# Moving operands of a hybrid decoder step laid out in rows of 2304 bytes, with a 4 KB DMA ring for GpSimd

## The chip, the cores and the metric

The kernel runs on one core of a Trainium2 chip. The metric is the device time of one execution in microseconds (us); the median of three runs of the kernel before is 1835.51 us (1834.74 to 1837.76). The profile is one execution taken by the hardware profiler.

## What is computed

One step of a decoder layer for 256 prompt tokens and 8 sample tokens (264 columns), all in float32: an RMS norm, one large input projection, three groups of heads, an output projection, the residual and a final norm.

```python
h = rms_norm(x, norm_w)
z = h @ w_in                                   # 4096 x 14368
qa, ka, va, ga, ub, gb, qc, kc, vc, gc, ac, bc = split_cols(z)
oa = combine_patterns([dilated_pattern(...) for w, d in A_PATTERNS])   # attention, 8 heads
ob = pool_mix(...)                                                     # causal pooling
oc = rms_norm(gated_delta(...), delta_norm_w)                          # delta rule, 16 heads
mix = concatenate([oa * silu(ga), ob * silu(gb), oc * silu(gc)])
y = rms_norm(x + mix @ w_out, final_norm_w)
```

The caches of keys and values are also copied through, shifted by one row.

## The kernel before

Both projections run as one stream of TensorE work. An output tile has 128 rows and 264 columns (`NT`), and there are 113 tiles of the input projection and 32 of the output projection. Each sums over 32 contraction tiles, here called k tiles. To keep float32 accuracy, every operand is split in an upper part and a lower part in the type float32r: a k tile of an output tile takes three matmuls (upper weights by upper x, upper weights by lower x, lower weights by upper x), lines 540, 541 and 542 of `emit_main`. I call the three a triple. The first output tile, `ab`, takes two matmuls instead (L535 to L538).

The moving operand of a triple comes from `rhs`. In the input projection it is row k of the tiles `xh` (upper) and `xl` (lower), each of 32 rows of 264 floats, so a row has 1056 bytes and the next starts 1056 bytes on. In the output projection it is row k of the mixed heads: `mixc0` to `mixc15`, one tile of 2 x 264 floats (2112 bytes) for each head of the delta rule, and the 16 rows of `mix2`, also of 2112 bytes; in both the lower part lies 1056 bytes behind the upper part.

Where a row lies follows from the sizes of what is allocated before it in a partition of the on-chip memory. Before `xh` stand 16384 bytes of the ring in which GpSimd's DMA descriptors are kept, 128 bytes of constants, 8 weight tiles of 4096, 3 raw tiles of 8192, the arena of 11776 floats, `small` of 1600 floats and 16 tiles of 2112 bytes: 161152 bytes, which is 128 modulo 256. `xl` lies 33792 bytes behind it, also at 128. Since 1056 is 32 modulo 256, row k of `xh` and of `xl` starts at 128 + 32 k modulo 256: eight places, one after the other. By the same count `mixc0` starts at 127360 (128 modulo 256), each next tile 64 further, and `mix2` takes the place of `xl`. So the upper parts of the output projection start at 128, 192, 0 and 64 in turn, and their lower parts 32 behind. The weights' tiles start at 128 modulo 256 for every matmul, before and after.

ScalarE makes the upper part of the weights and VectorE the lower one, chunk by chunk (8 k tiles), from three raw buffers that SyncE (SP) loads; `HB = 4` chunks of split weights may be ready. All else (convolutions, the delta rule's chains, attention, pooling) is written as generators. `step` lets each go on as far as a table of estimated engine times (`Model`) says that VectorE and ScalarE have time beside the stream, and as far as `get_all` finds room in the arena. So the order of the instructions on all engines is fixed when the program is built; a different size of the arena can change it. SP issues nearly all DMAs in one queue, in that order. GpSimd issues twelve small loads of constants and states.

Of the kernel before, what the change touches and what calls it, by code (L numbers as in the profile page):

```python
# [11 lines left out]
P = 128  # L12
NP = 256            # prompt tokens
NB = 8              # sample tokens (one per sequence)
NT = NP + NB
NK = 32             # contraction tiles of the model width
KC = 8              # contraction tiles per chunk
# [10 lines left out]
def tile_plan():  # L28
    """Order of the output tiles of the input projection: (kind, index)."""
    plan = [("ab", 0)] + [("k", h) for h in range(CH)]  # L30
    for h in range(CH):
        plan += [("q", h), ("v", h), ("g", h)]
    for h in range(AH):
        plan += [("qa", h), ("ka", h), ("va", h), ("ga", h)]
    for g in range(4):
        plan += [("u", 2 * g), ("u", 2 * g + 1), ("gb", 2 * g), ("gb", 2 * g + 1)]
    return plan
# [37 lines left out]
class Model:  # L75
    """Estimated times (us) of the engines' queues, and of every column's last write and last use."""
# [7 lines left out]
    def span(self, ap):  # L84
        """The quarters of the partitions and the columns of a tile (the kernel's inputs and outputs are not followed)."""
# [31 lines left out]
    def op(self, eng, dur, outs, ins):  # L117
        t = max(self.t[eng], self.ready(outs, ins))
        # engines take turns at a PSUM bank
# [24 lines left out]
class Meter:  # L144
    """An engine, with an estimate of the time that its instructions take (us)."""
# [33 lines left out]
class Chain:  # L179
    """A generator, the estimated time at which its last step is through, and its products yet to be issued."""  # L180
# [10 lines left out]
class Builder:  # L191
# [17 lines left out]
    def setup_space(self):  # L209
# [4 lines left out]
        self.XH = self.xp.tile([P, NK, NT], F32R, tag="xh", name="xh")  # L214
        self.XL = self.xp.tile([P, NK, NT], F32R, tag="xl", name="xl")
        self.r1 = [self.r1p.tile([P, 2, NT], F32, tag=f"r1_{h}", name=f"xr{h}") for h in range(CH)]
# [29 lines left out]
    def get_all(self, *sizes):  # L246
        """All of them or none, so that no two chains wait for each other's space."""
# [42 lines left out]
    def due(self, loaded):  # L290
        """Until a load can be expected to be there."""
        while not self.free and loaded > max(self.model.t["v"], self.model.t["pe"]) + SOON:
            yield
# [5 lines left out]
    def lose(self, t):  # L299
        """Time for ScalarE's tables."""  # L300
        self.s.used += t
        self.model.t["s"] += t

# [1 line left out]
    def mm(self, out, lhsT, rhs, start=True, stop=True):  # L305
        """A side product: it is issued inside a later chunk of the stream."""
# [14 lines left out]
    def flush(self, every=True):  # L321
        """The side products whose operands can be expected to be there."""
# [34 lines left out]
    def setup_const(self):  # L357
        d = self.d
        small = self.pool.tile([P, 1600], F32, name="small")
# [37 lines left out]
    def late_const(self):  # L397
# [4 lines left out]
        # halves: silu(z) = (tanh(z/2) + 1) * z/2  # L402
        self.ts(self.cw, self.cw, 0.5, ALU.mult)
        # buffers of the delta-rule phase
# [12 lines left out]
    def setup_stream(self):  # L417
        self.chunks = []      # (m, first k tile, number of k tiles, load index, offset in the load's tiles)
        self.loads = []       # (m, first k tile, number of k tiles, last chunk served, place, load that frees it)
# [36 lines left out]
    def emit_loads(self, limit=None):  # L456
        """The loads whose place is free."""
# [48 lines left out]
    def rhs(self, m, k):  # L506
        if m < N_IN:
            return self.XH[:, k, :], self.XL[:, k, :]
        t = self.mix[k]
        return t[:, 0:NT], t[:, NT:2 * NT]  # L510

    def main_bank(self, m):
        """The PSUM bank of an output tile, and the tile that had it before."""
# [4 lines left out]
    def emit_main(self, n):  # L518
# [3 lines left out]
        for i in range(nk):  # L522
# [8 lines left out]
            if m == 0:  # L531
                # rows 0 to 63: W's upper part by x; rows 64 to 127: its lower part by x's upper part
# [16 lines left out]
    def split_x(self, k):  # L549
        x = self.r1[k // 2][:, k % 2, :]  # L550
        w = self.nw[:, k:k + 1]
        self.act(self.XH[:, k, :], x, AF.Copy, scale=w)
        self.stt(self.XL[:, k, :], x, w, self.XH[:, k, :].bitcast(F32), ALU.mult, ALU.subtract)

    def square_x(self, q):
        """Squares of four of the k tiles, summed into self.ssum."""
# [51 lines left out]
    def ev_conv(self, kind, h, ps):  # L608
# [31 lines left out]
        if kind == "k":  # L640
            r = self.r1p.tile([P, 2 * NT], F32, tag=f"r1_{h}", name=f"kt{h}")
# [18 lines left out]
    def ev_ab(self, ps):  # L660
# [13 lines left out]
        # a_log -> -exp(a_log)  # L674
# [47 lines left out]
    def decay(self, h, gcb, D):  # L722
        """D[j, t, i] = exp(gc_i - gc_j) for i >= j, else 0."""
# [58 lines left out]
    def invert(self):  # L782
        """T = (I + A)^-1 of the 128 diagonal 32 x 32 blocks, one block per partition."""
# [32 lines left out]
    def assemble(self, hb):  # L816
        """E = T^T of the 128 x 128 tiles, from its 32 x 32 diagonal blocks, in place of U."""
# [90 lines left out]
    def delta(self, h, R, kd, D, o, S, X, sq):  # L908
# [65 lines left out]
        # 128 eps (sum q^2 + eps)  # L974
# [19 lines left out]
        # the last reader of k, U and E has been issued: their place takes the head's output  # L994
        mt = self.r1p.tile([P, 2 * NT], F32R, tag=f"r1_{h}", name=f"mixc{h}")
# [7 lines left out]
    def put_mix(self, mt, base, m, c0, c1):  # L1003
        hi, lo = mt[:, base + c0:base + c1], mt[:, base + NT + c0:base + NT + c1]
# [6 lines left out]
    def sample_tab(self):  # L1011
        """Columns by (head, sequence), then rows on all partitions: e^g, k2 e^g beta, k beta."""
# [72 lines left out]
    def sample_end(self):  # L1085
# [22 lines left out]
        for h in range(CH):  # L1108
# [3 lines left out]
            self.tt(mt[:, NT + NP:2 * NT], m, mt[:, NP:NT].bitcast(F32), ALU.subtract)  # L1112
# [56 lines left out]
    def have(self, k, buf):  # L1169
        """Row tile k of the mixed heads; those of attention come in two parts."""  # L1170
# [4 lines left out]
    def split_mix(self, k):  # L1175
# [3 lines left out]
        self.tt(t[:, NT:2 * NT], m.ap, t[:, 0:NT].bitcast(F32), ALU.subtract)  # L1179
# [164 lines left out]
    def ev_y(self, m, ps):  # L1344
        if m == 0:
            self.y = self.xp.tile([P, NK, NT], F32, tag="xh", name="y")
# [26 lines left out]
    def finish_early(self):  # L1373
        """What the last norm needs of the tiles but one."""
# [20 lines left out]
    def step(self, free=False):  # L1395
        """Each side chain goes on by a step, as far as VectorE and ScalarE have time beside the stream."""
# [87 lines left out]
    def build(self):  # L1484
# [8 lines left out]
        # TensorE's clock rises while it is busy  # L1493
# [19 lines left out]
        for n in range(len(self.chunks)):  # L1513
# [22 lines left out]
            if m >= N_IN:  # L1536
                if m == N_IN and c == 0:
                    self.mix2 = self.xp.tile([P, CH, 2 * NT], F32R, tag="xl", name="mix2")
# [59 lines left out]
ARENA = 11776  # L1598
# [8 lines left out]
# the first output tiles go side by side through the contraction, while x comes in  # L1607
# [4 lines left out]
# pieces of the caches' copy per load of weights: keys' tiles, delta rule, attention, pooling, output  # L1612
# [137 lines left out]
```

## Time and profile before

| | |
|---|---|
| time, median of 3 runs | 1835.51 us (1834.74 to 1837.76) |
| span of the profiled execution | 1828.2 us; its own time is not given apart from the span, and the median lies 7.3 us above the span |
| TensorE busy | 1801.3 us, 99% of the span |
| VectorE, ScalarE, GpSimd busy | 71%, 47%, 11% |
| chain of work that ended last | TensorE 88%, VectorE 5%, DMA 4% |
| granted TensorE clock from 130 to 1800 us | 1.00 (the 2.4 GHz level) |

Busy time of TensorE counts every matmul from its start to its modelled end, and successive matmuls overlap, so 99% tells that one always follows another and not how fast they follow. How fast is read from the starts.

### The profile page before, as it was taken

How to read it: one execution, taken by the hardware profiler on the slowest of the kernel's cores; microseconds unless marked ns; L12 is line 12 of the kernel's file. 1: busy time of each engine (PE TensorE's matmuls, PEld its weight loads, DVE VectorE, ACT ScalarE, POOL GpSimd, SP SyncE). 2: the span in 40 equal slices, each digit the busy share in tenths (PEclk: the TensorE clock that was granted, in tenths of full speed). 3: DMA queues.
4: the chain of work that ended last, by engine and by line, in shares of the span. 5: the costliest groups of instructions: out<-in, count | busy, mean ns of one | idle time of the engine just before them, and what ended most of it. 6: DMA issues, size and time to landing. Idle time of an engine off the chain costs nothing.

```text
span 1828.2 us, 38217 instructions
## 1 busy us (share of the span) xinstructions
PE 1801.3 (99%) x15120; PEld 1790.3 (98%) x15120; DVE 1298.7 (71%) x3155; ACT 850.3 (47%) x1442; POOL 192.8 (11%) x504
## 2 busy tenths in 40 slices
PE   9999999999999999999999999999999999999996
PEld 9999999999999999999999999999999999999995
DVE  7987879668789788787877778676655654444444
ACT  7644444455455455455544443434333444444442
POOL 1132560421011101111000000000000000000000
PEclk9999999999999999999999999999999999999998
DMA  9788897656787888879888888889888798888873
GB/s 322 263 289 295 272 234 260 237 198 234 262 327 269 286 305 313 304 267 319 323 312 306 313 308 297 284 283 333 306 299 288 274 339 302 295 294 303 297 240 118
DMA packets 109380, 519.66 MB, mean 284 GB/s; under 512 B 25408, under 2 KB 35872, under 8 KB 70272
## 3 DMA queue, kind: packets, MB, share of 16 engines
q1 hardware_dynamic: 108624, 516.71, 80.5%
q8 instruction: 118, 1.93, 0.4%
q0 software_dynamic: 432, 0.50, 0.1%
q14 instruction: 62, 0.51, 0.1%
q10 hardware_dynamic: 144, 0.02, 0.0%
HBM read 499.67 MB, written 152.50 MB: 357 GB/s over the span
## 4 chain that ended last, share of the span: by engine, by line
PE 88%; DVE 5%; DMA 4%; issue 1%; ACT 1%; SPq 1%; DVEq 0%; ACTq 0%
PE mps L540 27%; PE mps L541 27%; PE mps L542 27%; PE sps L307 4%; DVE arena L174 3%; DMA raw<-win 3%; DVE wl L174 2%; PE sps L311 1%; PE sps L541 1%; PE sps L540 1%; PE sps L542 1%; SPq L158 1%; DVE y L174 1%; DMA o_ds<-arena 0%; ACT wh L174 0%
## 5 line engine op out<-in xcount | busy, mean ns | idle before, releaser
L540 PE MATMUL mps<-xh,wh 128*128 128x264 f32 x3456 | 995.3, 288 | 2.0 <-ACT wh L174 2.0
L542 PE MATMUL mps<-xh,wl 128*128 128x264 f32 x3456 | 979.9, 284 | 1.7 <-DVE wl L174 1.6
L174 DVE TENSOR_TENSOR wl<-raw,wh 128x1024 fp32r<-128x1024 f32 (+1 forms) x581 | 704.5, 1214 | 389.7 <-ACT wh L174 382.4
L541 PE MATMUL mps<-xl,wh 128*128 128x264 f32 x3456 | 980.2, 284 | 0.0
L174 ACT CAST wh<-raw 128x1024 fp32r<-128x1024 f32 (+2 forms) x586 | 604.8, 1036 | 611.2 <-PE mps L541 471.7
L540 PEld LDWEIGHTS mps<-xh,wh 128*128 128x128 f32 x3456 | 652.1, 189 | 3.7 <-ACT wh L174 2.5
L541 PEld LDWEIGHTS mps<-xl,wh 128*128 128x128 f32 x3456 | 651.7, 189 | 0.2
L542 PEld LDWEIGHTS mps<-xh,wl 128*128 128x128 f32 x3456 | 648.8, 188 | 2.5 <-DVE wl L174 2.5
L174 DVE SCALAR_TENSOR_TENSOR arena<-arena 128x128 f32<-128x128 f32 (+5 forms) x882 | 264.6, 356 | 10.9 <-DMA arena<-s_k 4.2
L174 ACT ACTIVATE arena<-arena 128x128 f32<-128x128 f32 (+7 forms) x319 | 119.3, 401 | 143.3 <-DVE arena L174 140.8
L542 PE MATMUL mps<-mix,wl 128*128 128x264 f32 x512 | 145.7, 284 | 0.0
L542 PE MATMUL mps<-mixc,wl 128*128 128x264 f32 x512 | 145.7, 284 | 0.0
L540 PE MATMUL mps<-mixc,wh 128*128 128x264 f32 x512 | 145.5, 284 | 0.0
L540 PE MATMUL mps<-mix,wh 128*128 128x264 f32 x512 | 145.5, 284 | 0.0
L541 PE MATMUL mps<-mixc,wh 128*128 128x264 f32 x512 | 144.9, 283 | 0.0
L541 PE MATMUL mps<-mix,wh 128*128 128x264 f32 x512 | 144.8, 283 | 0.0
L174 POOL COPY arena<-arena 128x8 f32<-128x8 f32 (+5 forms) x192 | 67.8, 376 | 450.7 <-DVE arena L174 392.8
L540 PEld LDWEIGHTS mps<-mix,wh 128*128 128x128 f32 x512 | 96.2, 188 | 0.0
L540 PEld LDWEIGHTS mps<-mixc,wh 128*128 128x128 f32 x512 | 96.2, 188 | 0.0
L542 PEld LDWEIGHTS mps<-mixc,wl 128*128 128x128 f32 x512 | 96.1, 188 | 0.0
L542 PEld LDWEIGHTS mps<-mix,wl 128*128 128x128 f32 x512 | 96.1, 188 | 0.0
L541 PEld LDWEIGHTS mps<-mixc,wh 128*128 128x128 f32 x512 | 96.1, 188 | 0.0
(115 smaller groups left out, 1340.9 us busy)
## 6 DMA issues: line engine op xcount, KB each, us to landing
raw<-win SPq DMA_DIRECT2D x214, 1024.0 KB, 7.0
o_wk<-ck SPq DMA_DIRECT2D x128, 511.8 KB, 7.4
o_wv<-cv SPq DMA_DIRECT2D x128, 511.8 KB, 6.8
raw<-wout SPq DMA_DIRECT2D x58, 1024.0 KB, 5.3
arena<-kg SPq DMA_DIRECT2D x32, 320.0 KB, 6.7
arena<-vg SPq DMA_DIRECT2D x32, 320.0 KB, 7.1
arena<-sdT SPq DMA_DIRECT2D x32, 256.0 KB, 4.5
arena<-s_k SPq DMA_DIRECT2D x32, 256.0 KB, 4.5
```

The costliest lines, as they stand in the source:

```text
L158: return f(*a, **k)
L174: return f(*a, **k)
L307: self.put(lambda: self.t.matmul(out, lhsT=lhsT, rhs=rhs, start=start, stop=stop), out, [lhsT, rhs], 2)
L311: self.put(lambda: self.t.transpose(out, in_, self.ident[:k, :k]), out, [in_], 1)
L540: self.t.matmul(ps, lhsT=h[:, w], rhs=xh, start=(k == 0), stop=False)
L541: self.t.matmul(ps, lhsT=h[:, w], rhs=xl, start=False, stop=False)
L542: self.t.matmul(ps, lhsT=l[:, w], rhs=xh, start=False, stop=(k == NK - 1))
```

## The change

The rows of x and of the mixed heads get 576 floats (2304 bytes, nine times 256) each, with the upper part at the front and the lower part 288 floats (1152 bytes) behind it. `xh` and `xl` become two tiles `x0` and `x1` of 16 such rows, for the k tiles 0 to 15 and 16 to 31, with both parts in one row. `r1`, `kt`, `mixc` and `mix2` use the same rows. GpSimd's DMA ring shrinks from 16384 to 4096 bytes, and the arena grows from 11776 to 12480 floats, `small` from 1600 to 1632. Counted as above, the first row now starts at 4096 + 128 + 32768 + 24576 + 49920 + 6528 + 36864 = 154880, which is 0 modulo 256: every upper part starts at 0, every lower part at 128. Comments and empty docstrings also go, which only moves line numbers: lines 540, 541 and 542 become 543, 544 and 545.

```diff
-        self.XH = self.xp.tile([P, NK, NT], F32R, tag="xh", name="xh")
-        self.XL = self.xp.tile([P, NK, NT], F32R, tag="xl", name="xl")
-        self.r1 = [self.r1p.tile([P, 2, NT], F32, tag=f"r1_{h}", name=f"xr{h}") for h in range(CH)]
+        self.X = [self.xp.tile([P, NK // 2, ROW], F32R, tag=f"x{i}", name=f"x{i}") for i in range(2)]
+        self.r1 = [self.r1p.tile([P, ROW], F32, tag=f"r1_{h}", name=f"xr{h}")[:, :2 * NT].rearrange("p (a n) -> p a n", a=2)
+                   for h in range(CH)]
...
         if m < N_IN:
-            return self.XH[:, k, :], self.XL[:, k, :]
-        t = self.mix[k]
-        return t[:, 0:NT], t[:, NT:2 * NT]
+            t = self.X[k // 16][:, k % 16]
+        else:
+            t = self.mix[k]
+        return t[:, 0:NT], t[:, LO:LO + NT]
...
-        mt = self.r1p.tile([P, 2 * NT], F32R, tag=f"r1_{h}", name=f"mixc{h}")
+        mt = self.r1p.tile([P, ROW], F32R, tag=f"r1_{h}", name=f"mixc{h}")
...
-        self.tt(t[:, NT:2 * NT], m.ap, t[:, 0:NT].bitcast(F32), ALU.subtract)
+        self.tt(t[:, LO:LO + NT], m.ap, t[:, 0:NT].bitcast(F32), ALU.subtract)
...
-                    self.mix2 = self.xp.tile([P, CH, 2 * NT], F32R, tag="xl", name="mix2")
+                    self.mix2 = self.xp.tile([P, CH, ROW], F32R, tag="x1", name="mix2")
...
-ARENA = 11776
+ARENA = 12480
+ROW, LO = 576, 288
+SCRATCH = 4096
...
-    nc = _bacc.Bacc("TRN2", target_bir_lowering=False, num_devices=1)
+    nc = _bacc.Bacc("TRN2", target_bir_lowering=False, num_devices=1,
+                     dynamic_dma_scratch_size=SCRATCH)
```

No instruction is added or taken away, but the larger arena moves some. From the inversion of the delta rule's blocks (`assemble`, some 340 us into the program) to the end of the delta rule, the side chains find room at other moments. On SP, where the sample chains load their states (`sdT`, `s_k`, `s_q`), the program before has:

```order
L158 DMA raw_80<-win 128x2048
L158 DMA o_wk<-ck 16x8188
L158 DMA raw_81<-win 128x2048
L158 DMA arena<-sdT 128x512
L158 DMA arena<-s_k 128x512
L158 DMA s_q<-small 128x2x4
L158 DMA arena<-s_q 128x512
L158 DMA raw_79<-win 128x2048
```

and the changed one has in the same place:

```order
L158 DMA raw_80<-win 128x2048
L158 DMA o_wk<-ck 16x8188
L158 DMA arena<-sdT 128x512
L158 DMA arena<-s_k 128x512
L158 DMA s_q<-small 128x2x4
L158 DMA arena<-s_q 128x512
L158 DMA raw_81<-win 128x2048
L158 DMA arena<-sdT 128x512
```

The load of the weights' buffer `raw_81` now stands behind the four DMAs of a sample chain. On VectorE, in `assemble`, the piece of the difference (- before, + changed; `kt_1709` and `kt_1985` are two heads' tiles, `wl` a lower part of weights) reads:

```order
 L174 TENSOR_TENSOR arena<-mps_103,small 128x256
 L174 TENSOR_TENSOR arena<-mps_103,small 128x8
+L174 COPY arena<-sps_104 32x256
 L174 SCALAR_TENSOR_TENSOR arena<-sps_106,arena 128x128
 L174 SCALAR_TENSOR_TENSOR arena<-sps_107,arena 128x128
 L174 TENSOR_TENSOR wl_77<-raw_81,wh_73 128x1024
 L174 SCALAR_TENSOR_TENSOR arena<-arena,small 128x288 x3
-L174 TENSOR_SCALAR kt_1709<-sps_104 64x2x64
-L174 TENSOR_SCALAR kt_1985<-sps_104 64x2x64
-L174 TENSOR_TENSOR wl_78<-raw_81,wh_74 128x1024
```

A copy of the next group of blocks moves ahead, and the end of the group before it comes later.

## Rows read from the trace of the kernel before

**Rows 1.** The page: span, and busy time, share and instructions of engines.

```profile
span 1828.2 us, 38217 instructions
...
PE 1801.3 (99%) x15120; PEld 1790.3 (98%) x15120; DVE 1298.7 (71%) x3155; ACT 850.3 (47%) x1442; POOL 192.8 (11%) x504
```

**Rows 2.** The page's chain of work that ended last, by engine.

```profile
PE 88%; DVE 5%; DMA 4%; issue 1%; ACT 1%; SPq 1%; DVEq 0%; ACTq 0%
```

**Rows 3.** Groups by line: count, busy us, mean ns, idle before.

```profile
L540 PE MATMUL mps<-xh,wh 128*128 128x264 f32 x3456 | 995.3, 288 | 2.0 <-ACT wh L174 2.0
...
L542 PE MATMUL mps<-mix,wl 128*128 128x264 f32 x512 | 145.7, 284 | 0.0
...
L174 ACT ACTIVATE xh<-xr,small 128x264 fp32r<-128x264 f32 x32 | 15.3, 509 | 3.1 <-DMA xr<-xT 1.9 <-DMA small<-nw 1.2
```

**Rows 4.** Stretches: length, busy time and count by engine, granted clock, DMA.

```profile
130.00:460.00 330.00, 330.00 (x3065) 327.42 (x3065) 257.76 (x635) 153.87 (x273) 112.61 (x287) 1.00 0.75 247
460.00:970.00 510.00, 503.62 (x4156) 500.94 (x4155) 418.62 (x1251) 258.89 (x546) 50.79 (x140) 1.00 0.84 298
970.00:1450.00 480.00, 479.16 (x3925) 475.89 (x3924) 328.48 (x899) 197.25 (x305) 5.75 (x17) 1.00 0.85 300
1450.00:1800.00 350.00, 350.00 (x2879) 350.00 (x2878) 171.02 (x182) 152.64 (x183) 0.00 (x0) 1.00 0.81 285
```

**Rows 5.** Timeline, input projection: k tiles 0 to 8 of output tile 7, L540 alone.

```profile
85.88 0.28 PE L540 MATMUL mps<-xh,wh 128*128 128x264 f32 x1
...
86.23 0.28 PE L540 MATMUL mps<-xh,wh 128*128 128x264 f32 x1
...
86.60 0.29 PE L540 MATMUL mps<-xh,wh 128*128 128x264 f32 x1
...
86.96 0.28 PE L540 MATMUL mps<-xh,wh 128*128 128x264 f32 x1
...
87.32 0.28 PE L540 MATMUL mps<-xh,wh 128*128 128x264 f32 x1
...
87.68 0.28 PE L540 MATMUL mps<-xh,wh 128*128 128x264 f32 x1
...
88.05 0.28 PE L540 MATMUL mps<-xh,wh 128*128 128x264 f32 x1
...
88.41 0.29 PE L540 MATMUL mps<-xh,wh 128*128 128x264 f32 x1
...
88.78 0.28 PE L540 MATMUL mps<-xh,wh 128*128 128x264 f32 x1
...
1432.55 0.28 PE L540 MATMUL mps<-xh,wh 128*128 128x264 f32 x1
```

**Rows 6.** Timeline, output projection: k tiles 0 to 4 of output tile 116, L540 alone.

```profile
1470.47 0.28 PE L540 MATMUL mps<-mixc,wh 128*128 128x264 f32 x1
...
1470.83 0.28 PE L540 MATMUL mps<-mixc,wh 128*128 128x264 f32 x1
...
1471.19 0.29 PE L540 MATMUL mps<-mixc,wh 128*128 128x264 f32 x1
...
1471.57 0.28 PE L540 MATMUL mps<-mixc,wh 128*128 128x264 f32 x1
...
1471.93 0.28 PE L540 MATMUL mps<-mixc,wh 128*128 128x264 f32 x1
...
1808.09 0.28 PE L540 MATMUL mps<-mix,wh 128*128 128x264 f32 x1
```

**Rows 7.** Timeline of SP's queue from 400 to 432 us.

```profile
407.19 0.33 SPq L158 DMA_DIRECT2D raw<-win  x1
412.10 0.33 SPq L158 DMA_DIRECT2D arena<-sdT  x1
...
416.44 0.38 SPq L158 DMA_DIRECT2D raw<-win  x1
```

**Rows 8.** Timeline of GpSimd: the first of its late DMAs.

```profile
70.76 0.57 POOL L158 DMA_DIRECT2D arena<-scT  x1 [64.56 <-DVE arena L174]
```

More of the change, by code (lines that the diff above doesn't have):

```diff
@@ L358, in setup_const @@
         d = self.d
-        small = self.pool.tile([P, 1600], F32, name="small")
+        small = self.pool.tile([P, 1632], F32, name="small")
         off = [0]
@@ L551, in split_x @@
         w = self.nw[:, k:k + 1]
-        self.act(self.XH[:, k, :], x, AF.Copy, scale=w)
-        self.stt(self.XL[:, k, :], x, w, self.XH[:, k, :].bitcast(F32), ALU.mult, ALU.subtract)
+        hi, lo = self.rhs(0, k)
+        self.act(hi, x, AF.Copy, scale=w)
+        self.stt(lo, x, w, hi.bitcast(F32), ALU.mult, ALU.subtract)
     def square_x(self, q):
@@ L640, in ev_conv @@
         if kind == "k":
-            r = self.r1p.tile([P, 2 * NT], F32, tag=f"r1_{h}", name=f"kt{h}")
+            r = self.r1p.tile([P, ROW], F32, tag=f"r1_{h}", name=f"kt{h}")
             self.kt[h] = r
@@ L1003, in put_mix @@
     def put_mix(self, mt, base, m, c0, c1):
-        hi, lo = mt[:, base + c0:base + c1], mt[:, base + NT + c0:base + NT + c1]
+        hi, lo = mt[:, base + c0:base + c1], mt[:, base + LO + c0:base + LO + c1]
         self.s.copy(out=hi, in_=m.ap[:, c0:c1])
@@ L1111, in sample_end @@
             self.s.copy(out=mt[:, NP:NT], in_=m)
-            self.tt(mt[:, NT + NP:2 * NT], m, mt[:, NP:NT].bitcast(F32), ALU.subtract)
+            self.tt(mt[:, LO + NP:LO + NT], m, mt[:, NP:NT].bitcast(F32), ALU.subtract)
             if h % 4 == 3:
@@ L1345, in ev_y @@
         if m == 0:
-            self.y = self.xp.tile([P, NK, NT], F32, tag="xh", name="y")
+            self.y = self.xp.tile([P, NK, NT], F32, tag="x0", name="y")
             self.acc = [self.now(NT), self.now(NT)]
```

## The prediction

> **What bounds the kernel now.** I read the page first. TensorE is busy for 1801.3 of 1828.2 us [rows 1], and the chain that ended last runs through TensorE for 88% of the span [rows 2]. Busy time says nothing of pace, so I went on to stretches. From 1450 to 1800 us TensorE runs nothing but the output projection's matmuls: 2879 in 350.00 us, one every 121.6 ns, with not a nanosecond idle and at the granted clock of 1.00, the 2.4 GHz level [rows 4]. If one of the 264 columns went in at each cycle, that would be 110 ns. So by this estimate some 11 ns of each matmul is something else, and since TensorE waits for nothing there, I looked for it in the operands.
>
> The timeline shows that it depends on the row. From one L540 to the next is one triple. In the first full period of the input projection the triples take .35, .37, .36, .36, .36, .37, .36, .37 us [rows 5]; one row is too coarse (10 ns), so I averaged the triples between which no side product stands, from the first L540 of those rows to the last: 3067 triples, 265 to 423 for each of eight residues of k. By the start of the row modulo 256 bytes (128 + 32 k) they take, in ns: 128: 358.8; 160: 363.5; 192: 365.1; 224: 358.1; 0: 359.2; 32: 367.6; 64: 360.9; 96: 370.5. Rows k, k + 8, k + 16 and k + 24 agree within 1 ns, though they differ in every higher address bit. The mean of the eight is 363.0.
>
> In the output projection the pattern repeats after four k tiles: .36, .36, .38, .36 us [rows 6], over 926 triples from the first to the last of those rows 360.0 (upper part at 128, lower at 160), 363.0 (192, 224), 372.7 (0, 32) and 364.3 (64, 96). Row k and row k + 4 use different slices of the weights and agree within 0.1 ns, so the weights' slice is not the cause, and neither is the place in the chunk. The mean is 365.0.
>
> **The pace after the change.** No row of before has the upper part at 0 and the lower at 128, so this cost must be put together. The simplest rule is that each matmul pays by the start of its own moving row. A third of an input triple prices one matmul at each residue, and two upper and one lower predict the output's four triples: 128/160 gives 2 x 119.6 + 121.2 = 360.4 (measured 360.0); 192/224 gives 2 x 121.7 + 119.4 = 362.8 (363.0); 64/96 gives 2 x 120.3 + 123.5 = 364.1 (364.3). Three of four within 0.4 ns. The fourth fails: 0/32 gives 2 x 119.7 + 122.5 = 362.0, and 372.7 was measured, 10.7 more. So the rule holds mostly, and something in which neighbours take part can break it.
>
> With the rule, 0/128 gives 2 x 119.7 + 119.6 = 359.1 ns for each triple, everywhere. In the input projection 112 tiles have 32 triples: 3584 x (363.0 - 359.1) = 14.0 us. In the output projection 32 tiles: 1024 x (365.0 - 359.1) = 6.0 us. (Output tile 0, with 64 matmuls, is left out.) Together 20.0 us.
>
> Bounds of this unknown: above, the interaction of the 0/32 row on every triple, 359.1 + 10.7 = 369.8, a loss of 3584 x 6.8 + 1024 x 4.8 = 29.3 us. Below, the fastest triple that any residue shows made up of single matmuls: the output's L541 at 160 between two rows at 128 starts its successor after 116.4 ns on average, so three such give 349.2, a gain of 3584 x 13.8 + 1024 x 15.8 = 65.6 us. I take the own-start rule, since three of four rows obey it.
>
> By the Trainium skill ("TensorE: Matmul & The Clock Gate", section "Wait — 56ns, not 53.3ns?") a warm matmul follows the last after N / 2.4 + 2.5 ns, an estimate of 112.5 ns here, and the sum by it would be 3584 x 25.5 + 1024 x 27.5 = 119.6 us less; no row of this trace comes near it.
>
> **What of it reaches the end.** Where the chain runs through VectorE, DMA and SP, a faster TensorE only waits more. I count the gain in TensorE's share of the chain, 88% [rows 2]: 20.0 x 0.88 = 17.6 us. The stretch to watch is the delta rule, 460 to 970 us: TensorE idles 6.4 us of 510 there and VectorE is busy 82% [rows 4].
>
> **What moves.** The larger arena reorders the side chains from `assemble` to the end of the delta rule. Instructions and their shapes are the same, so the price is one of waits alone. TensorE's idle time from 130 to 1450 us is 0.0 + 6.4 + 0.8 us [rows 4]. Taking the 6.4 us away altogether is the most to gain; a second helping of the same is my bound for the loss. On SP the load into `raw_81` now stands behind the four DMAs of a sample chain. Before, it was issued at 407.19 us, the chain's first DMA at 412.10 and the next weights' load at 416.44 [rows 7]. If the chain's first DMA waits as long as before, this load comes up to 9.2 us late, and behind it the splits of its two chunks on ScalarE and VectorE, for which TensorE waits. The cover is the stream's own lead: three split chunks, 3 x 8 triples x 363 ns = 8.7 us of TensorE work. Uncovered, it costs up to 9.2 us once. I take 0 for the whole reordering and keep -6.4 and +6.4 for the range.
>
> **The 4 KB ring.** GpSimd issues nine loads at the start and then idles 64.56 us before the next three [rows 8]. Should a small ring make a load wait for the one before it, that idle time hides it; those late three feed the first convolutions, in a stretch where TensorE doesn't wait (330.00 of 330.00 us busy from 130 to 460 us, [rows 4]). Price 0; without that cover a few us at worst.
>
> **The writers.** ScalarE and VectorE write as many elements as before: 32 upper parts of x at 509 ns [rows 3]. ScalarE is busy 47% [rows 1]; price 0, and were each 10% slower, 1.6 us.
>
> **Sum.** 1828.2 - 17.6 = 1810.6 us of span. The median lies 7.3 us over the span, which the change doesn't touch: 1817.9, say 1818 us.
>
> **Rivals.**
>
> *Slower: the two parts of a row disturb each other.* As in the 0/32 rows, an upper part at 0 alternating with a lower part elsewhere costs extra. For it: the only measured triples of the output projection with the upper part at 0 are the slowest. Against it: 0 followed by 0 is among the fastest in the input projection. At the full 10.7 ns the time is 1835.5 + 29.3 = 1865 us, and TensorE, being slower, then bounds all the more, so no share comes off. It decides from 20.0 us / 4608 triples = 4.3 ns of extra on a triple.
>
> *Much faster.* All triples settle at the fastest matmul seen: 65.6 x 0.88 = 57.7 us less, 1778 us. For it: the new pattern is the same for every k, as in the long runs at 128. Against it: the row at 0 shows 119.7, not 116.4; and VectorE's stretches would end first more often.
>
> *No change: the start of a row is not the cause.* The pattern by k would be due to the order of the three matmuls or to the clocks, and would come back in another form with the same mean; the time is 1835 us, give or take the reordering. For it: the time of a triple depends on neighbours too, as 0/32 shows. Against it: the agreement of rows 8 apart and of three output triples with input prices. The Trainium skill ("SBUF — State Buffer", section "Specifications (TRN2)") gives lines of 16 bytes, with a penalty for each crossing. Every row here starts at a multiple of 32 and crosses 66 such lines, before and after, so that rule alone would foresee this rival; the trace disagrees, with 358.1 to 370.5 ns at starts that the rule treats alike.
>
> **Chances.** The forecast (faster by 10 to 28 us) 0.46; much faster 0.15; no change 0.14; slower by the interaction, in full or in part, 0.25. A measurement of this kernel tells about 0.2% (3.7 us) from no change. So faster 0.62, same 0.13, slower 0.25. The range: from the much faster case at 1778, to most of the interaction, 1856; the forecast's own is 1808 to 1826 (two thirds to one and a half of 17.6 us, and the reordering's 6.4 within it).
>
> **What would show each step.** From 1450 to 1800 us no triple should depend on k any more. Its matmuls should follow at 119.7 ns where it was 121.6: about 2925 in 350 us. The output's three lines should each start the next at a constant distance. A span shorter by less than TensorE's pace accounts for, with more idle TensorE between 460 and 970 us, would show the absorbed share. GpSimd's loads should take 0.5 us each, as now. I am wrong if the triples come out over 363 ns, or if idle time in the delta rule grows by more than 6 us; the first would be the interaction, the second the reordering.

## The result and the profile after

The changed kernel takes 1857.71 us (median of 4 runs, 1855.78 to 1858.34) against 1835.51. The ratio of their runs is put at 1.0115, interval 1.0101 to 1.013 (the quotient of these two medians is 1.0121). By the medians it is slower by 22.2 us, where 1818 us and a gain were forecast, and lies above the range, which ended at 1856.

The page of the profile after: span, busy time, the chain's shares by engine, and the groups of two of the three lines of a triple. (The removed comments move lines 540, 541 and 542 to 542, 543 and 544; the text on the change put them one too far.)

```profile
span 1856.6 us, 38231 instructions
...
PE 1823.0 (98%) x15120; PEld 1811.8 (98%) x15120; DVE 1299.6 (70%) x3155; ACT 849.1 (46%) x1442; POOL 195.3 (11%) x504
...
PE 80%; DVE 9%; DMA 7%; issue 2%; ACT 2%; SPq 0%; POOL 0%; DVEq 0%; ACTq 0%; POOLq 0%
...
L542 PE MATMUL mps<-x,wh 128*128 128x264 f32 x3456 | 1005.5, 291 | 0.3 <-ACT wh L174 0.3
L543 PE MATMUL mps<-x,wh 128*128 128x264 f32 x3456 | 992.0, 287 | 0.0
...
L543 PE MATMUL mps<-mixc,wh 128*128 128x264 f32 x512 | 146.7, 287 | 0.0
...
L542 PE MATMUL mps<-mixc,wh 128*128 128x264 f32 x512 | 145.9, 285 | 0.0
```

Against [rows 1] the span grows by 28.4 us: TensorE is busy 21.7 us longer with the same 15120 matmuls, and its idle time grows from 26.9 to 33.6 us. (The spans differ by more than the medians do: the profiled execution of before was a quick one. The one after took 1858.34 us, 1.7 above its span, so most of the 7.3 us that the prediction put around the span was scatter between executions.) The same stretches as in [rows 4], with the columns busy time and count of PE, PEld, DVE, ACT and POOL, granted clock, DMA share and GB/s, show both parts:

```profile
0.00:130.00 130.00, 127.17 (x994) 125.67 (x995) 108.39 (x180) 83.66 (x130) 23.68 (x60) 0.97 0.80 284
130.00:460.00 330.00, 330.00 (x3035) 327.53 (x3034) 255.81 (x626) 150.74 (x270) 110.63 (x283) 1.00 0.76 248
460.00:970.00 510.00, 497.05 (x4032) 493.48 (x4031) 407.49 (x1213) 254.79 (x544) 53.50 (x142) 0.99 0.81 289
970.00:1450.00 480.00, 480.00 (x3900) 477.31 (x3899) 326.46 (x913) 191.60 (x287) 7.51 (x19) 1.00 0.85 297
1450.00:1800.00 350.00, 350.00 (x2860) 349.74 (x2859) 175.11 (x201) 153.00 (x192) 0.00 (x0) 1.00 0.83 296
```

**Pace.** Where TensorE never idles, fewer matmuls go through: 3035 for 3065, 3900 for 3925, 2860 for 2879 (2925 were expected). Averaged from the timeline as in the prediction, an input triple takes 367.4 ns whatever its k (367.1 to 368.0; 3053 triples), an output triple 366.7 (366.4 to 367.0; 926). A step of the output projection, one triple from L542 to L542:

```profile
1470.45 0.28 PE L542 MATMUL mps<-mixc,wh 128*128 128x264 f32 x1
1470.58 0.29 PE L543 MATMUL mps<-mixc,wh 128*128 128x264 f32 x1
1470.70 0.28 PE L544 MATMUL mps<-mixc,wl 128*128 128x264 f32 x1
1470.82 0.28 PE L542 MATMUL mps<-mixc,wh 128*128 128x264 f32 x1
```

The dependence on k is gone, as foreseen, but at the slow end: 3584 x 4.4 + 1024 x 1.7 = 17.5 us lost. In the first 130 us there are 30 matmuls fewer than before (994 for 1024), at a granted clock of 0.97 for 1.00. The slower pace makes some 12 of the 30. The clock there comes and goes between executions of one kernel (1.00 and 0.97 in the two profiles of another kernel below, with 1010 and 1011 matmuls), and I don't count the rest as an effect.

**Idle time.** From 460 to 970 us TensorE idles 12.95 us instead of 6.4. The waits of TensorE in that stretch (us, times, longest), first of the kernel before, then of the changed one:

```profile
PE mps L540 <- ACT wh L174: 1.8, 1, 1.8
PE sps L311 <- DVE arena L174: 1.7, 2, 1.4
PE mps L542 <- DVE wl L174: 1.4, 2, 0.8
PE sps L307 <- DVE arena L174: 1.2, 2, 0.9
```

```profile
PE sps L308 <- DVE arena L174: 5.5, 6, 2.0
PE sps L312 <- DVE arena L174: 2.8, 3, 2.4
PE sps L312 <- ACT arena L174: 2.1, 1, 2.1
PE sps L312 <- POOL arena L174: 1.5, 1, 1.5
PE sps L308 <- ACT arena L174: 1.0, 2, 0.7
```

TensorE now waits only in the side products (`mm` and `tr`, L308 and L312), for VectorE's, ScalarE's and GpSimd's parts of the delta rule: 12.9 us, where it was 2.9 plus 3.2 for the weights' split. The granted clock falls with it: it is 0.50 (the 1.2 GHz level) from 656.3 to 659.3 and from 916.0 to 918.5 us, with TensorE idle for 2.4 us between 650 and 665 and for 2.1 us between 905 and 925. Before had one such place in this stretch (0.50 from 607.8 to 610.6 us).

### The profile page after: what moved, and what is told of

Its sections match the earlier page's. It is cut to its first block, busy times and chain, and to the rows that moved or that the text cites. A ratio compares the mean times of both kernels' runs of the same rounds, so it can differ in the third digit from the quotient of the medians.

```text
span 1856.6 us, 38231 instructions
## 1 busy us (share of the span) xinstructions
PE 1823.0 (98%) x15120; PEld 1811.8 (98%) x15120; DVE 1299.6 (70%) x3155; ACT 849.1 (46%) x1442; POOL 195.3 (11%) x504
## 4 chain that ended last, share of the span: by engine, by line
PE 80%; DVE 9%; DMA 7%; issue 2%; ACT 2%; SPq 0%; POOL 0%; DVEq 0%; ACTq 0%; POOLq 0%
PE mps L542 24%; PE mps L543 24%; PE mps L544 24%; DVE arena L174 5%; DMA raw<-win 4%; PE sps L308 4%; DVE wl L174 3%; DMA o_ds<-arena 2%; ACT wh L174 1%; PE sps L542 1%; PE sps L543 1%; PE sps L544 1%; PE sps L312 1%; ACT arena L174 1%; DMA arena<-s_k 1%
## 5 line engine op out<-in xcount | busy, mean ns | idle before, releaser
L542 PE MATMUL mps<-x,wh 128*128 128x264 f32 x3456 | 1005.5, 291 | 0.3 <-ACT wh L174 0.3
L543 PE MATMUL mps<-x,wh 128*128 128x264 f32 x3456 | 992.0, 287 | 0.0
L544 PE MATMUL mps<-x,wl 128*128 128x264 f32 x3456 | 985.2, 285 | 0.0
L542 PEld LDWEIGHTS mps<-x,wh 128*128 128x128 f32 x3456 | 655.2, 190 | 1.8 <-ACT wh L174 0.6
L544 PEld LDWEIGHTS mps<-x,wl 128*128 128x128 f32 x3456 | 656.6, 190 | 0.2 <-DVE wl L174 0.2
L543 PEld LDWEIGHTS mps<-x,wh 128*128 128x128 f32 x3456 | 654.7, 189 | 0.2
L174 DVE SCALAR_TENSOR_TENSOR arena<-arena 128x128 f32<-128x128 f32 (+4 forms) x882 | 264.0, 354 | 10.5 <-DMA arena<-s_k 3.7
L542 PE MATMUL mps<-mix,wh 128*128 128x264 f32 x512 | 145.9, 285 | 0.0
L542 PE MATMUL mps<-mixc,wh 128*128 128x264 f32 x512 | 145.9, 285 | 0.0
L544 PE MATMUL mps<-mixc,wl 128*128 128x264 f32 x512 | 145.2, 284 | 0.0
L544 PE MATMUL mps<-mix,wl 128*128 128x264 f32 x512 | 145.2, 284 | 0.0
L174 POOL COPY arena<-arena 128x8 f32<-128x8 f32 (+5 forms) x192 | 72.6, 400 | 458.2 <-DVE arena L174 384.8
L542 PEld LDWEIGHTS mps<-mix,wh 128*128 128x128 f32 x512 | 96.6, 189 | 0.0
L542 PEld LDWEIGHTS mps<-mixc,wh 128*128 128x128 f32 x512 | 96.6, 189 | 0.0
L543 PEld LDWEIGHTS mps<-mix,wh 128*128 128x128 f32 x512 | 96.2, 188 | 0.0
L544 PEld LDWEIGHTS mps<-mixc,wl 128*128 128x128 f32 x512 | 96.2, 188 | 0.0
```

The source lines that it names most:

```text
L174: return f(*a, **k)
L542: self.t.matmul(ps, lhsT=h[:, w], rhs=xh, start=(k == 0), stop=False)
L543: self.t.matmul(ps, lhsT=h[:, w], rhs=xl, start=False, stop=False)
L544: self.t.matmul(ps, lhsT=l[:, w], rhs=xh, start=False, stop=(k == NK - 1))
```

## Experiments

Numbers per triple are averages from the timeline as above, between whose matmuls no side product stands. The first two kernels split the change. In their traces the instructions of every engine come in the order that the text says: the layout alone in that of before, the order alone in that of the change.

**The layout alone**: the changed kernel with the old arena, and so with the old order on every engine.

```diff
-ARENA = 12480
+ARENA = 11776
```

> The rows of 2304 bytes and the 4 KB ring as in the change, but the arena at its old 11776 floats, so that the order of all instructions is that of the kernel before. Theory A (the matmuls' pace takes most of the loss): triples at about 367 ns as after the change, idle TensorE from 460 to 970 us back near the 6.4 us of before, time 1851 us (3584 x 4.4 + 1024 x 1.7 ns = 17.5 us over before, less what waits already there take up). Theory B (the new order of the side chains takes most of it): 1840 us or less. Theory C (slower rows shift the waits, the order has no part): the same 1857 us as the change.

**The order alone**: the kernel before with the new arena and ring, and so with the new order.

```diff
-ARENA = 11776
+ARENA = 12480
+SCRATCH = 4096
```

> The old rows, with the 4 KB ring and the arena of 12480 floats, so that the order of all instructions is that of the change while the rows start where they did modulo 256. Theory A: triples as before (363.0 and 365.0 ns), some 6 us more idle TensorE from 460 to 970 us, time 1838 to 1842 us. Theory B: 1850 us or more. Theory C: 1836 us.

The layout alone takes 1849.2 us, ratio 1.0073 (1.0053 to 1.0092); the order alone 1843.6 us, 1.0034 (1.0019 to 1.005). The product, 1.0107, is within the interval of the change. The layout alone is thus some 13 us slower, where 17.5 were worked out from its pace. The input's triples with a side product or a wait, which that count leaves out, scatter by more than the difference (236.2 to 243.0 us in six traces of the old order), so it isn't resolved here. The stretches from 460 and from 1450 us, layout alone first:

```profile
460.00:970.00 510.00, 503.45 (x4104) 500.31 (x4103) 410.07 (x1217) 258.43 (x547) 49.61 (x142) 1.00 0.83 293
1450.00:1800.00 350.00, 350.00 (x2860) 349.74 (x2859) 174.88 (x196) 153.57 (x194) 0.00 (x0) 1.00 0.84 297
```

```profile
460.00:970.00 510.00, 494.24 (x4050) 489.58 (x4048) 407.80 (x1212) 254.57 (x543) 56.65 (x138) 0.99 0.81 294
1450.00:1800.00 350.00, 350.00 (x2876) 349.87 (x2875) 174.62 (x194) 154.60 (x192) 0.00 (x0) 1.00 0.83 297
```

The layout brings the slow triples (2860; 367.2 and 366.7 ns) and no new idle time (6.55 us); the order brings the idle time (15.8 us, and two places with a granted clock of 0.50, as in the change) and leaves the triples (363.0 and 365.0). So the two causes are separate.

**Which places are slow.** Four k tiles to each pair of places, upper and lower part from 0/32 to 0/224 and 128/160; the rest is the changed kernel.

```diff
-        return t[:, 0:NT], t[:, LO:LO + NT]
+            a, b = PLACES[k // 4]
+            return t[:, a:a + NT], t[:, b:b + NT]
```

> The changed kernel, but each k tile of x has its own places in its row of 2304 bytes, four k tiles to a pair: upper part at 0 with the lower one at 32, 64, 96, 128, 160, 192 and 224 modulo 256, and the upper at 128 with the lower at 160. The mixed heads stay at 0 and 128. Theory P (a triple's time is set by the pair of places of its two parts): each block of four has one time of its own, 372.7 ns for 0/32, 367.3 for 0/128, 360.0 for 128/160, as in the rows of before and after with these pairs; the others lie anywhere from 356 to 373. Theory S (each matmul pays by its own start): 362.0 for 0/32, 359.1 for 0/128, 360.4 for 128/160, 359.7 to 363 for the rest. Theory N (the place has no part, a regular row costs 367): all blocks within 2 ns of 367.

1858.44 us (one run). The eight blocks' triples average 366.6 to 367.7 ns, as a regular row would by the third of the expectations, but within a block single rows take 361.8 to 374.1. 0/32 gives 367.3 (not 372.7), 128/160 gives 366.8 (not 360.0): a pair of places has no price of its own, and my rival's price for 0/32 falls with the own-start rule.

**The weights moved** by 64 bytes in the kernel before; all that lies behind them moves by 256, so the rows keep their places modulo 256.

```diff
+        self.pool.tile([P, 16], F32, name="pad0")
         self.H = [...]
         self.L = [...]
+        self.pool.tile([P, 48], F32, name="pad1")
```

> The kernel before with all weights' tiles 64 bytes further (192 modulo 256, not 128) and everything that moves at its old place modulo 256. Theory W (a matmul's reads of its moving rows and the next one's reads of weights get in each other's way, so the distance between the two places counts): the pattern over k turns by two rows; the input's slowest triple goes from start 96 (370.5 ns) to 160, the output's slowest pair from 0/32 (372.7) to 64/96, the means stay at 363 and 365. Theory M (only the moving rows' own places count): the same times at the same rows as before, within 1 ns.

1836.4 us (one run), nearly the same means (362.7, 365.0), but the output's pattern turns by one row: 364.0, 360.0, 363.3, 372.7 ns for upper parts at 128, 192, 0, 64, so the slow row is now 64/96. Its distance from the weights is what 0/32 had. In the input, seven of the eight rows come within 1.3 ns of the row that had their distance before, and the eighth, at 160, takes 367.1 instead of 370.5, so that it is not the slowest, as was expected, but second to the row at 96 (367.5). By their own places the eight miss by 2.1 to 9.4 ns. In this sequence of rows it is the distance that counts.

**Drifts.** Eight rows of each kind, all with both parts at one place modulo 256, each next row the named number of bytes further; the last kernel drifts by 32 with the lower part 128, -32, 32 or 64 ahead.

> The changed kernel with the rows of x packed by a table of places: both parts of a k tile at the same place modulo 256, which from one k tile to the next moves by 0 bytes (k 0 to 7), by -32 (8 to 15), by 128 (16 to 23) and by 64 (24 to 31). The mixed heads stay as in the change. Theory L (the reads of a matmul's moving row and of the next one's weights get in each other's way; where the relation of the two starts comes back triple after triple the two settle into one rhythm of 366.7 ns, whatever the places; a drift of the relation keeps them from it): 366.7 for drift 0, something else for the other three, 363 to 365 if a drift of -32 or 64 does what +32 did before. Theory S (each matmul pays by its own start): 359 for drift 0 and for 128, 363 for -32 and for 64.

> As the kernel before this one, with drifts of 96, -64, -96 and 16 bytes from one k tile to the next. Theory L: four different values, none of them the settled 366.7 unless the drift is too small to keep the two streams apart (16 bytes). Theory S: 363 for each of the first three, whose places run through the same multiples of 32; 364 for 16 bytes.

> As the kernels before, all with a drift of 32 bytes from one k tile to the next, and with the lower part ahead of the upper one by 128, -32, 32 and 64 bytes modulo 256 in the four blocks. Theory L: all four clear of 366.7, since the relation changes with each triple; how far depends on the steps inside the triple. Theory S: 363 in each block.

1852.94, 1851.53 and 1852.62 us (one run each). Averages over the eight rows, ns: drifts of 0, -32, 128, 64: 364.5, 365.0, 365.2, 363.4; of 96, -64, -96, 16: 364.5, 365.1, 364.4, 365.5; the lower part 128, -32, 32, 64 ahead: 366.2, 365.8, 364.7, 365.1. All between the input of before (363.0) and the changed kernel, with scatter from row to row (359 to 374), and in the drift of 0 too (363.3 to 366.7), where every row has the same places. The drift of 0 gave neither the 366.7 nor the 359 ns of the expectations.

**The weights drift** instead of the rows: the weights' slices lie 544 bytes apart instead of 512, first in the changed kernel, then in the kernel before, where rows and weights then drift together and their distance stays.

```diff
-        self.H = [self.pool.tile([P, KC * 128], F32R, name=f"wh{i}") for i in range(HB)]
+        self.H = [self.pool.tile([P, KC, WS], F32R, name=f"wh{i}")[:, :, 0:128] for i in range(HB)]
...
+WS = 136
```

> The changed kernel with all moving rows at 0 and 128 as it has them, but the eight slices of each weights' tile 544 bytes apart in place of 512, so that the weights move by 32 bytes modulo 256 from one k tile to the next (the ring takes 2048 bytes to make room). Theory L: the relation drifts again, though on the other side; triples near the 363 ns of before, time 4608 x 4 ns = 18 us under the change, 1836 to 1846 us with the new order of the side chains still in it. Theory K (only the sequence of the moving rows' places counts): 367 ns and the 1857 us of the change.

> The kernel before, its order and its rows of x, with the weights' slices 544 bytes apart, so that in the input projection a weights' slice and its moving row now start at the same place modulo 256 for every k. Relation (the distance between a moving row and the weights decides): the input's triples lose their dependence on k (358.1 to 370.5 ns before) and come to one value, between 364.5 (the rows of the same kind in the run with drifts of 0, -32, 128 and 64) and 366.7 (what the changed kernel's rows settle at), so 5 to 13 us slower, 1842 to 1850. Own start: nothing changes, the same pattern by k with a mean of 363.0, 1836 to 1838.

In the changed kernel this gives 1845.92 us, ratio 1.0042 (1.0028 to 1.0056): the triples fall to 364.6 and 364.2 and some 12 us come back with the rows of x untouched. In the kernel before the input's pattern goes (364.2 to 366.1 by k, mean 364.9), the output gets another one (mean 368.3), and the kernel is slower: 1844.69 us, 1.0047 (1.0029 to 1.0064). Own starts, which didn't change there, would have left it at 363.0.

**The constant distance.** The layout alone again, with the weights' tiles moved by 64, 32, 96, 128 and 192 bytes. The two pads add up to 256 bytes each time, so in these five kernels the rows lie at identical addresses (256 further than in the layout alone), and only the weights differ. Every triple of a kernel then has the same two distances.

> The layout alone (arena of 11776 floats) with all weights' tiles 64 bytes further, at 192 modulo 256. If any constant distance settles at one rhythm: 366.7 ns per triple in the output and about 367.4 in the input, as without the move, and 1847 to 1851. If the size of the constant distance counts: another value, between 359 and 373, and a time of 1820 to 1870.

> The layout alone with the weights' tiles 32 bytes further: upper parts 96, lower parts 224 from the weights modulo 256. Prices by distance that add up (each matmul at a third of the input triple of the kernel before that has its distance): 2 x 119.4 + 123.5 = 362.2 ns per triple. A rhythm in which the neighbours take part: one constant value in undisturbed output tiles that need not be that sum, out of those seen so far (360.0, 364.4, 366.7, 373.3).

> The weights' tiles 96 bytes further: upper parts 32, lower parts 160 from the weights. Prices that add up: 2 x 121.2 + 122.5 = 364.9 ns. Rhythm: one of the values seen so far, not that sum.

> The weights' tiles 128 bytes further: upper parts 0, lower parts 128 from the weights, the two distances of the changed kernel exchanged. Prices that add up: 2 x 119.6 + 119.7 = 358.9 ns, some 1817 us. Rhythm: one of the values seen so far; if only distances modulo 128 count, 366.7 again and 1849 us.

> The weights' tiles 192 bytes further: upper parts 192, lower parts 64 from the weights, the two distances of the run with 64 exchanged. Prices that add up: 2 x 120.3 + 121.7 = 362.3 ns. Rhythm: one of the values seen so far; if only distances modulo 128 count, 360.0 and 364.4 as in the run with 64, and 1830 to 1836 us.

| weights moved by | us | input triple | output triple | prices that add up |
|---|---|---|---|---|
| 0 | 1849.2 | 367.2 | 366.7 | 359.1 |
| 32 | 1843.79 (one run) | 366.5 | 366.7 | 362.2 |
| 64 | 1832.16 (one run) | 362.1 | 364.4 | 363.7 |
| 96 | 1841.16 (one run) | 364.3 | 366.7 | 364.9 |
| 128 | 1838.15 (one run) | 365.4 | 365.3 | 358.9 |
| 192 | 1841.68, ratio 1.003 | 364.7 | 364.4 | 362.3 |

Prices that add up miss by up to 8.1 ns and in no order. "A value seen before" fails too, for 128 (365.4) and 96 (363.3). What the tiles show is a rhythm: with 64, whole output tiles run at 360.0 ns and others at 364.4; with 96, at 363.3 and 366.7; with 0, most at 366.7 and some at up to 373.3. With 32 the output alternates between 357.5 and 375.9 ns from one k to the next, as the starts of L544 there show (.36, .37, .36, .38 us):

```profile
1600.02 0.28 PE L544 MATMUL mps<-mixc,wh 128*128 128x264 f32 x1
...
1600.38 0.29 PE L544 MATMUL mps<-mixc,wh 128*128 128x264 f32 x1
...
1600.75 0.28 PE L544 MATMUL mps<-mixc,wh 128*128 128x264 f32 x1
...
1601.11 0.29 PE L544 MATMUL mps<-mixc,wh 128*128 128x264 f32 x1
...
1601.49 0.28 PE L544 MATMUL mps<-mixc,wh 128*128 128x264 f32 x1
```

The triples of one kernel, all with the same two distances modulo 256, need not take the same time: in the output with 192 they take 378, 350, 365 ns in turn, with 64 they take 360, 365, 369, and with 128 the pattern comes back after five. Since 32 k tiles are no multiple of three or five, these patterns don't belong to certain k.

**Timed, and in the change itself.** The kernel with 64 again, in twelve runs; the change with its own arena and order and the weights moved by 64; and two kernels with rows of 2336 bytes, in which the output's rows drift by 32 with both parts at one place: in both projections (weights unmoved, `small` of 1600 floats so that the first row starts at 128; the diff), or in the output alone, with the rows of x as in the kernel with 64.

```diff
-ARENA = 12480
-ROW, LO = 576, 288
+ARENA = 11776
+ROW, LO = 584, 320
```

> The kernel of the one look at 1832.16 us again (2304-byte rows, arena of 11776 floats, weights at 192 modulo 256), now timed. The pace of its trace, 362.1 and 364.4 ns per triple against 363.0 and 365.0, is worth 3584 x 0.9 + 1024 x 0.6 = 3.8 us: a ratio of 0.998 and some 1832 to 1835 us. If the one look was a fast one of its spread: within 0.1% of the kernel before.

> The change as it is, with its arena and its order, and only the weights' tiles 64 bytes further. Pace and order add up: 1832.2 plus 6 to 7 us for the order, 1838 to 1840 us, so some 18 us under the changed kernel. If the order costs nothing once TensorE is faster: 1832 to 1834. If it costs more because TensorE waits more: over 1842.

> The changed kernel with rows of 2336 bytes (32 modulo 256) with the lower part 1280 bytes behind, and the arena of 11776 floats: in both projections both parts then start at 128 + 32 k, as in the input projection before. Relation and own start alike: every triple as in the input projection before, a mean of 363.0, so the output gains 1024 x 2.0 = 2.1 us on the kernel before, 1834 to 1836. If what is found is only that each long sequence settles somewhere of its own: input and output triples anywhere between 362 and 366.7, 1833 to 1850.

> The best of both: rows of x as in the change with the weights' tiles at 192 (362.1 ns per triple), rows of the mixed heads of 2336 bytes (drift 32, both parts at one place, 362.5 ns), arena of 11776 floats. If each projection keeps its own pace: 3584 x 0.9 + 1024 x 2.5 = 5.8 us under the kernel before, a ratio of 0.997. If the weights' place changes the pace of the output rows as well: 364 to 366 ns there, and 1832 to 1835 us.

- Layout with 64: 1836.5 us, ratio 1.0 (0.9987 to 1.0014). The single run of 1832.16 us was at the low end of its scatter (1831.67 to 1839.95). The pace is again 362.1 and 364.4, but the 3.8 us that it should be worth against the kernel before don't show.
- Change with 64: 1833.38 us, 0.999 (0.9978 to 1.0001), some 24 us below the change.
- All rows drifting: 1833.5 us, 0.9981 (0.9968 to 0.9993); 363.0 and 362.5 ns, averaged over the places as before. Expected 363.0 in both.
- Output rows alone drifting: 1833.79 us, 0.9984 (0.9969 to 0.9998); 362.1 and 362.5 ns. Of 5.8 us, 2.9 came.

The last two beat both kernels, by little. The stretches of the layout with 64, then of the change with 64:

```profile
460.00:970.00 510.00, 499.42 (x4121) 494.86 (x4119) 414.12 (x1235) 257.84 (x545) 49.92 (x139) 1.00 0.83 296
1450.00:1800.00 350.00, 350.00 (x2884) 350.00 (x2883) 170.96 (x183) 151.32 (x181) 0.00 (x0) 1.00 0.82 292
```

```profile
460.00:970.00 510.00, 494.63 (x4057) 490.04 (x4056) 407.66 (x1216) 255.24 (x544) 54.48 (x138) 0.99 0.82 295
1450.00:1800.00 350.00, 350.00 (x2919) 350.00 (x2918) 176.66 (x194) 155.03 (x190) 0.00 (x0) 1.00 0.84 297
```

The change's order still costs idle time (15.4 against 10.6 us, and 7.75 in the single run of the layout with 64), so the order's cost has not gone. But in the profiled execution its output projection runs in the other rhythm, 360.0 ns per triple over all 926 triples against 364.4 (2919 matmuls against 2884), with rows and weights at the same places modulo 256 (modulo 512 the rows lie 256 further, as the larger arena moves them by 2816 bytes). That is worth 1024 x 4.4 = 4.5 us and about covers the idle time; I had expected 1838 to 1840. That the places alone do not choose the rhythm shows within one kernel too. Two executions of the layout with 64, the first L544 of output tile 10 and that of tile 11, 32 triples apart, with no idle time between them; the single run first:

```profile
122.80 0.28 PE L544 MATMUL mps<-x,wh 128*128 128x264 f32 x1
...
134.47 0.28 PE L544 MATMUL mps<-x,wh 128*128 128x264 f32 x1
```

```profile
122.74 0.28 PE L544 MATMUL mps<-x,wh 128*128 128x264 f32 x1
...
134.26 0.28 PE L544 MATMUL mps<-x,wh 128*128 128x264 f32 x1
```

11.67 us / 32 = 364.7 ns in one, 11.52 / 32 = 360.0 in the other, for the same instructions at the same addresses.

The traces also show where the two part. Just before the ninth k tile of output tile 9 both run at 360.0 ns per triple. There, in the single run alone, one L546 is followed after 0.22 us instead of 0.11 to 0.13, without a side product; the triple takes 464 ns, and from there to the end of output tile 10 the mean is 364.4, while the other execution stays at 360.0. The single run first:

```profile
113.96 0.28 PE L544 MATMUL mps<-x,wh 128*128 128x264 f32 x1
114.08 0.28 PE L545 MATMUL mps<-x,wh 128*128 128x264 f32 x1
114.20 0.39 PE L546 MATMUL mps<-x,wl 128*128 128x264 f32 x1
114.42 0.28 PE L544 MATMUL mps<-x,wh 128*128 128x264 f32 x1
```

```profile
114.10 0.28 PE L544 MATMUL mps<-x,wh 128*128 128x264 f32 x1
114.22 0.28 PE L545 MATMUL mps<-x,wh 128*128 128x264 f32 x1
114.35 0.28 PE L546 MATMUL mps<-x,wl 128*128 128x264 f32 x1
114.46 0.28 PE L544 MATMUL mps<-x,wh 128*128 128x264 f32 x1
```

In the three traces of weights moved by 64 (55, 55 and 51 stretches of 18 or more triples between which stands neither a side product nor such a break) the two halves of every stretch agree within 1.2 ns. So here a rhythm, once taken, held until the stream was interrupted.

## Why the prediction was wrong

**What failed: the own-start rule.** The prediction priced a matmul by the start of its own moving row and put 0/128 at 359.1 ns. It came out at 367.4 and 366.7. The prices were averages over rows that were only ever met in a moving sequence, and they held neither in a constant one nor with the weights moved. Behind it stood a reading that cleared the weights: rows k and k + 4 agreed over different slices. But all slices lie 512 bytes apart and start at 128 modulo 256, so that their agreement says nothing of the weights' place. The start of a moving row counts by its distance from the weights' start (moving the weights alone turns the pattern, changes the pace, or takes the loss away), and the pace of a sequence belongs to the sequence as a whole. The sign was there: the row 0/32 missed the rule by 10.7 ns, and I let three rows that agreed decide against one that didn't. Both signs of being wrong that the prediction named came: triples over 363 ns, and 6.6 us more idle time in the delta rule.

**What the prediction had right.** That the layout works on TensorE's pace and on nothing else of it: the layout alone shows no new idle time. That dependence on k would go. That the order's price lies in the delta rule and is one of waits (and of the clock that fell with them). The ring and the writers at 0: TensorE is busy 330.00 of 330.00 us up to 460 us, GpSimd's late load is issued at 73.59 us after 67.41 us of idle time (2.8 us later than in [rows 8], and nothing waits for it), and the upper parts of x take 508 ns as in [rows 3]. The late load of weights: it is issued at 417.64 us, 10.4 us later than in [rows 7], and the stream's lead hid it. Only some 4 us of this come from the order: the layout alone issues the same load at 413.69 us.

```profile
L174 ACT ACTIVATE x<-xr,small 128x264 fp32r<-128x264 f32 x32 | 15.3, 508 | 2.7 <-DMA xr<-xT 1.5 <-DMA small<-nw 1.2
```

```profile
73.59 0.56 POOL L158 DMA_DIRECT2D arena<-scT  x1 [67.41 <-DVE arena L174]
```

```profile
409.30 0.34 SPq L158 DMA_DIRECT2D raw<-win  x1
...
417.64 0.38 SPq L158 DMA_DIRECT2D raw<-win  x1
```

**What was mis-sized: the reordering.** Taken at 0 with 6.4 us as its bound, it cost 0.34% (0.19 to 0.5), some 6 us, about that bound. The place that I named (the late weights' load) was not the one that paid: the side products were, since TensorE runs them in order with the stream and stood before them until VectorE, ScalarE or GpSimd was through. The 7.3 us between span and median were no constant either: the execution profiled after the change took 1.7 us more than its span. And the share of 88% for what reaches the end was put to no test, since there was no gain.

**The rivals.** The slower one had the sign and its condition (4.3 ns per triple; 8.3 and 7.6 ns over 359.1 were measured), but its reason, a bad pair of parts, was refuted. "No change" had the cause wrong. The estimate of 112.5 ns per matmul by the Trainium skill ("TensorE: Matmul & The Clock Gate", section "Wait — 56ns, not 53.3ns?") came out in no trace: the triples of 350 to 379 ns in the output are 117 to 126 ns per matmul.

**What stays open.** Why certain distances go with certain rhythms, and which rhythm a stream takes after an interruption. The traces show changes behind side products and behind the short break in output tile 9; no run here varies one alone. The Trainium skill ("SBUF — State Buffer", section "Who interferes with whom") gives TensorE two independent read ports, one for the moving operand and one for the load of weights. By that the weights' place should not matter to the pace; the runs disagree, with 366.5 and 362.1 ns for rows of x at identical addresses over weights at 160 and at 192. Where in the path the two meet isn't shown. It is also not shown that only the address modulo 256 counts: the alternation of 357.5 and 375.9 ns goes with rows 2304 bytes apart, which differ in the next address bit.

## What to carry to other kernels

A price per operand that is averaged out of a moving sequence holds in that sequence; before a layout is made uniform, time the uniform one, because it may make every step the slow one. When a dense TensorE stream without idle time runs slower than it could, move the weights' tiles by 32 to 192 bytes first: it is a change of two lines, and here 64 bytes were worth 24 us in 1858 for the changed kernel. They were worth nothing for the kernel before (1836.4 us, one run). And when a buffer's size feeds a scheduler, change the two apart: here the arena and the ring, without the rows, cost 6 of the 22 us.

## What was unexpected of the hardware

- The same instructions on the same addresses have more than one steady pace (360.0 or 364.4 ns per triple), without a nanosecond of idle time and at the granted clock of 1.00; a break of 0.1 us stood between the two.
- The values 360.0, 366.7 and 373.3 ns, at which every triple takes the same time, are 864, 880 and 896 cycles at 2.4 GHz, 16 cycles apart for three matmuls of 264 columns. The others (363.3, 364.4, 365.3) are means over patterns of two, three and five triples.
- The place of the stationary operand changes the spacing of matmuls, as that of the moving one does: 32 bytes further, with the rows at identical addresses, a triple took 362.1 ns instead of 366.5.
